# A ring of their own for the raw tiles of the seven-product pairs in the input projection, and an ordinary pair between them

## The chip, the cores and the metric

The kernel runs on one core of one Trainium2 chip. The metric is the device time of one execution in microseconds; three executions of the kernel before gave 2222.35, 2225.07 and 2228.02 us, so the median is 2225.07 us.

## The reference, cut to what matters

The program is a trunk of two layers on 256 tokens of width 2048, all in float32. What the change touches is the first matrix product of each layer, `h @ w_in`: 256 x 2048 by 2048 x 6144. Its columns are the queries, keys and values of two kinds of attention heads.

```python
def hybrid_mixer(h, layer, w_in, w_o, ...):
    proj = h @ w_in                       # (256, 2048) @ (2048, 6144)
    q_sb, k_sb, v_sb, q_d, k_d, v_d = jnp.split(proj, offs, axis=-1)   # 1024 columns each
    o_sb = rms_norm(stick_breaking_attention(q_sb, k_sb, v_sb), sb_out_norm)
    q_d, k_d = partial_rope(q_d), partial_rope(k_d)
    o_d = rms_norm(differential_attention(q1, q2, k1, k2, v_d, lam), diff_subln) * (1 - lam_init)
    return concatenate([o_sb, o_d]) @ w_o

def reference(x, ...):
    for l in range(2):
        x = x + rms_norm(hybrid_mixer(rms_norm(x, pre_mix_norm[l]), ...), post_mix_norm[l])
        x = x + rms_norm(swiglu(rms_norm(x, pre_ffn_norm[l]), ...), post_ffn_norm[l])
    return x
```

## The kernel before, in words

**Split numbers.** Every matrix product is made of three matmuls. A float32 weight tile `raw` is split by ScalarE (ACT) into a rounded part `hi` and by VectorE (DVE) into the rest, `lo = raw - hi`; the activations are split in the same way. `product` (L919 to L924) then issues high by high, high by low and low by high on TensorE (PE), each 128 x 128 stationary against 512 columns.

**Tiles and pairs.** A weight tile holds two blocks of 128 rows, a "K pair" `kp`, and 512 columns: 128 x 1024 numbers, 512 KB. The projection has 12 column chunks of 512, taken two at a time, so it has six column pairs (`PAIRS`, n = 0 to 5), and for each of them it walks through the eight K pairs in the order `IN_ORDER` (n = 0: 0 to 7). An ordinary K pair (`eight_in`) needs two rows x two token tiles x two columns = 8 products, 24 matmuls. A K pair of `IN_SEVEN`, 4 and 5, in the column pairs n = 1 to 4 (`IN_NOW`) is done by a Strassen-like scheme with 7 products, 21 matmuls (`seven_in`, `seven_products`). For this the first and the second column's raw tiles, `g` and `u`, are combined and split on DVE and ACT (`mixed_weights`, L213 on): one addition of 512 columns (L226); the split of `u` into `hi` and `lo` (L222, L223); a difference of 512 columns (L229); an addition of 1024 columns (L230); and the splits of the two results into `Th` and `Tl`. The first tile `g` is also split in the ordinary way (L247, L249). Nearly all of these read or rewrite the raw tiles in place, so both stay in use until the last `Tl`.

**Rings.** All raw tiles of the projection, ordinary or not, come from one ring, `raw`, of 4 buffers. `hi` and `lo` are rings of 6 buffers, three K pairs. `Th` and `Tl` have 2 buffers each in the pool `sums`, which also holds the combined activations (`sh`, `sl`). After the last seven-product pair of a layer `sums` is given up and `late` takes its place. A tile that wants a buffer waits for the last reader of the tile that was in it.

**Queues.** Weight loads go through SyncE's (SP's) DMA queue one after the other (L199 for `raw`), written in the order of `weight_order`, which follows `IN_ORDER`. A load whose buffer isn't free holds up the loads behind it. `weights(i, LOOKAHEAD)` asks for loads and splits four tiles, two K pairs, ahead of the one being multiplied. A scheduler then orders the instructions of each engine; on the chip each engine takes them in that order.

**PSUM banks and attention.** PSUM has eight banks. Four, `acc`, hold the sums of the column pair in work; three, `b`, and one, `o`, serve attention, that runs between the projection's matmuls. A seven-product scheme needs four more sums (`p1`, `p6`, `p7`, `q5`), and takes the three `b` banks and the `o` bank for them. After the last seven-product pair `shared_part` empties these: L959 copies `p1` on ACT, L960 to L963 are additions on DVE that read `p6`, `p7`, `q5` and `q5`.

**The planner.** Attention is written as generators that `tick()` advances; a tick is called once per six matmuls in `eight_in` and four times in seven products, so every K pair has 4 ticks and a column pair 32. `burst` holds the ticks between which the extra sums have the banks; `clear(n)` tells whether n ticks fit before or after it, and after it two more ticks (`SETTLE`) must pass. `banks_for` hands out the `b` banks. The scores of the differential heads (`diff_weights`, L625) take two `b` banks; `flip` transposes a column chunk of queries or keys (L841); `attend` (L546 to L550) multiplies by the values into the bank `o`, from which `norm_pair` makes `on` (L507). The output projection after n = 5 starts a K pair only when the heads that it needs are ready, and lets empty ticks pass until then.

Of the kernel before, what the change touches and what calls it, by code (L numbers as in the profile page):

```python
# [9 lines left out]
F32 = mybir.dt.float32  # L10
F32R = mybir.dt.float32r
# [6 lines left out]
P = 128  # L18
# [7 lines left out]
CW = 512  # L26
# [7 lines left out]
KP_O = (4, 5, 6, 7, 0, 1, 2, 3)  # L34
PAIRS = ((6, 8), (10, 7), (9, 0), (11, 2), (1, 3), (4, 5))
IN_SEVEN = (4, 5)
IN_ORDER = (0, 1, 4, 5, 6, 2, 3, 7)
IN_NOW = ((), IN_SEVEN, IN_SEVEN, IN_SEVEN, IN_SEVEN, ())
SETTLE = 2
SEVEN = (2, 4, 5, 6)  # L40
# [15 lines left out]
def weight_order():  # L56

    order = []

    def queue_pair(name, l, kp, c):  # L60
        order.append((name, l, kp, c))
        return len(order) - 1

    plan = []
    sevens, plain = set(), set()
    for l in range(L):
        lay = {"in": {}, "o": {}, "gate": {}, "up": {}, "down": {}}
        for n, (ca, cb) in enumerate(PAIRS):
            for kp in IN_ORDER if n else range(KT // 2):
                lay["in"][ca, kp] = queue_pair("w_in", l, kp, ca)  # L70
                lay["in"][cb, kp] = queue_pair("w_in", l, kp, cb)
                if kp in IN_NOW[n]:
                    plain.add(lay["in"][cb, kp])
        order_o = [(c, kp) for kp in KP_O for c in (0, 1)]
        order_o += [(c, kp) for c in (2, 3) for kp in range(KT // 2)]
        lay["order_o"] = order_o
        for c, kp in order_o:
            lay["o"][c, kp] = queue_pair("w_o", l, kp, c)
        for c in range(FF // CW):
            for kp in FIRST_ORDER if c == 0 else range(KT // 2):  # L80
                lay["gate"][c, kp] = queue_pair("w_gate", l, kp, c)
                lay["up"][c, kp] = queue_pair("w_up", l, kp, c)
                if kp in (FIRST_SEVEN if c == 0 else SEVEN):
                    sevens.add(lay["up"][c, kp])
        for half in range(2):
            for kp in range(FF // P // 2):
                for c in (2 * half, 2 * half + 1):
                    lay["down"][c, kp] = queue_pair("w_down", l, kp, c)
                if kp in DOWN_SEVEN:
                    sevens.add(lay["down"][2 * half + 1, kp])  # L90
        plan.append(lay)
    return order, plan, sevens, plain
# [14 lines left out]
class Rooms:  # L107


    PASSING = ("a", "ah", "al", "w", "ra", "rb")  # L110
    SUMS = ("Th", "Tl", "sh", "sl")
    LATE = ("mixs", "x", "w_late")

    def __init__(self, tc, name):
# [14 lines left out]
    def tile(self, *args, **kw):  # L129
        for tags, pool in ((self.PASSING, self.passing), (self.SUMS, self.sums), (self.LATE, self.late)):  # L130
            if kw["tag"] in tags:
                return pool.tile(*args, **kw)
        return self.lasting.tile(*args, **kw)
# [7 lines left out]
def kernel(  # L141
# [18 lines left out]
    wpool = ctx.enter_context(tc.tile_pool(name="wpool", bufs=1))  # L160
# [5 lines left out]
    def bank(name):  # L166
        return ps.tile([P, CW], F32, tag="b", bufs=3, name=name)
# [9 lines left out]
    order, plan, sevens, plain = weight_order()  # L177
# [6 lines left out]
    def fetch(upto):  # L184
        while len(raws) < min(upto, len(stream)):
            i = len(raws)
            for j in range(i, min(i + EARLY + 1, mix_raw[3])):
                if j in sevens and j not in sums:
                    summed(j)
            if i in sevens:  # L190
                raws.append(sums[i])
                continue
            if i + 1 in sevens:
                g = mix_raw[0].tile([P, 2, CW], F32, tag="G", bufs=mix_raw[1], name=f"G{i}")
                loads.append(nc.sync.dma_start(g, stream[i]))
                raws.append(g)
                continue
            raw = wpool.tile([P, 2, CW], F32, tag="raw", bufs=4, name=f"raw{i}")
            loads.append(nc.sync.dma_start(raw, stream[i]))  # L199
            raws.append(raw)  # L200

# [2 lines left out]
    def summed(i):  # L204

        sums[i] = mix_raw[0].tile([P, 2, CW], F32, tag="T", bufs=mix_raw[2], name=f"T{i}")
        loads.append(nc.sync.dma_start(sums[i], stream[i]))
        nc.gpsimd.dma_start(sums[i][:, 0, :], stream[i - 1][:, 0, :], accum_op=ALU.add)  # L208

    mix_pool = [None]  # L210
    mix_raw = [None, 0, 0, 0]

    def mixed_weights(i):  # L213

        g, u = raws[i - 1], raws[i]
        hi = wpool.tile([P, 2, CW], F32R, tag="hi", bufs=6, name=f"hi{i}")
        lo = wpool.tile([P, 2, CW], F32R, tag="lo", bufs=6, name=f"lo{i}")
        th = mix_pool[0].tile([P, 3, CW], F32R, tag="Th", bufs=2, name=f"Th{i}")
        tl = mix_pool[0].tile([P, 3, CW], F32R, tag="Tl", bufs=2, name=f"Tl{i}")

        def split(h, l, w):
            nc.scalar.activation(h, w, AF.Copy)  # L222
            nc.vector.tensor_tensor(out=l, in0=w, in1=h.bitcast(F32), op=ALU.subtract)  # L223

        if i in plain:
            nc.vector.tensor_tensor(out=u[:, 0, :], in0=g[:, 0, :], in1=u[:, 0, :], op=ALU.add)  # L226
        split(hi, lo, u)
        t2 = u[:, 1, :]
        nc.vector.tensor_tensor(out=t2, in0=t2, in1=u[:, 0, :], op=ALU.subtract)  # L229
        nc.vector.tensor_tensor(out=g, in0=g, in1=t2.unsqueeze(1).to_broadcast([P, 2, CW]), op=ALU.add)  # L230
        split(th[:, 2, :], tl[:, 2, :], t2)
        split(th[:, 0:2, :], tl[:, 0:2, :], g)
        t1, b22 = ((hi[:, k, :], lo[:, k, :]) for k in range(2))
        t3, t4, t2 = ((th[:, k, :], tl[:, k, :]) for k in range(3))
        return {"b22": b22, "t1": t1, "t2": t2, "t3": t3, "t4": t4}
# [188 lines left out]
    def banks_for(n, ticks, held=False):  # L424

        taken[:] = [until for until in taken if until > clock[0]]
        if len(taken) + n > 3 or not clear(ticks):
            return False
        taken.extend([math.inf if held else clock[0] + 2] * n)
        return True  # L430
# [4 lines left out]
    def start(gen, n=1):  # L435
        running.append([clock[0] + n, gen])
# [355 lines left out]
    def mixer_in(pool, l, rs, xT, mix, mixed):  # L792
# [7 lines left out]
        for n, cc in enumerate(PAIRS):  # L800
            banks = [acc_bank(f"in{l}_{c}_{t}") for t in range(NT) for c in cc]
            mine = IN_NOW[n]
            w, toks = None, {}
# [24 lines left out]
            def flip(c, toks):  # L828
                kind, g = divmod(c, 2)
                st = heads[kind // 3, g]  # L830
                before = {(0, 0): (1, 0), (0, 1): (1, 1)}.get((kind // 3, g))
                while before and heads[before]["scored"] < 2:
                    yield 1
                key = "q" if kind in (0, 3) else "k"
                tT = st[key] = pool.tile([P, 4, S], F32, tag="qk", bufs=4, name=f"{key}T{l}_{c}")
                for t in range(NT):
                    while not banks_for(1, 2):
                        yield 1
                    pb = bank(f"qkT_ps{l}_{c}_{t}")
                    for j in range(4):  # L840
                        nc.tensor.transpose(pb[:, j * P : (j + 1) * P], toks[c, t][:, j * P : (j + 1) * P], ident)  # L841
                    nc.scalar.copy(tT[:, :, t * P : (t + 1) * P], pb.rearrange("p (h q) -> p h q", h=4))
                    yield 2
                st[key + "done"] = True
                if "qdone" in st and "kdone" in st:
                    if kind < 3:
                        start(stick_weights(pool, l, g, st))
                        start(attend(pool, "sb", l, g, st, mix, mixed))
                    else:
                        for j in range(2):  # L850
                            start(diff_weights(pool, l, g, st, j), 1 + 3 * j)
                        start(attend(pool, "df", l, g, st, mix, mixed))
# [3 lines left out]
            else:  # L856
                kps = IN_ORDER if n else tuple(range(KT // 2))
                extra = None
                burst[0] = clock[0] + 4 * kps.index(mine[0]) if mine and n else None
                for j, kp in enumerate(kps):  # L860
# [3 lines left out]
                    if kp in mine:  # L864
# [4 lines left out]
                        if kp == mine[-1]:  # L869
# [4 lines left out]
                            if n + 1 < len(PAIRS) and IN_NOW[n + 1]:  # L874
                                burst[0] = clock[0] + 4 * (len(kps) - 1 - j) + 4 * IN_ORDER.index(IN_NOW[n + 1][0])
                            else:
# [20 lines left out]
            wait = 3  # L897
            for c in cc:
                if c // 2 not in (2, 5):
                    start(flip(c, toks), wait if c // 2 < 3 else wait + 6 + 4 * len(IN_NOW[n + 1]))  # L900
                    wait += 3

    def seven_in(banks, extra, sums, xT, l, cc, kp, first, last):
# [65 lines left out]
    for l in range(L):  # L969
# [130 lines left out]
        for half in range(2):  # L1100
# [69 lines left out]
            for t in range(NT):  # L1170
# [4 lines left out]
                for c in cc:  # L1175
                    for kp in range(nkp - tail, nkp):
# [4 lines left out]
                        for kk in range(2):  # L1181
                            sh, sl = jh[:, kk, t * P : (t + 1) * P], jl[:, kk, t * P : (t + 1) * P]
# [65 lines left out]
```

## Time and profile before

| | before |
|---|---|
| median of three runs | 2225.07 us |
| the profiled execution, its own time | 2224.53 us |
| its span, first to last instruction | 2222.8 us |
| mean granted TensorE clock | 0.996 |
| busy: PE, DVE, ACT, POOL | 2192.6, 1862.7, 1354.5, 135.7 us |
| layer 0, column pairs n = 1 to 5 | about 47.6 to 306.0 us |
| layer 1, column pairs n = 1 to 5 | about 1156.8 to 1410.5 us |

The profile is of one execution. A line of a group gives source line, engine, operation, output <- inputs, count, then busy time and mean duration in ns, then the time that the engine was idle just ahead of these instructions, and what ended it. A line of the waits reads "who <- for whom: us in total, times, longest". A line of the timeline gives the start and the duration in us, and in brackets the idle time before it with its releaser. A line of the windows gives the window, its length, and each engine's busy time and number of instructions, then the granted clock, the share of DMA time and GB/s. Matmuls overlap their neighbours, so the distance of their starts, and not their duration, is what one costs.

### The profile page before, as it was taken

The numbers are of one execution on the slowest core, as the hardware profiler recorded it, in microseconds if no ns is written. First come the engines' busy times: TensorE is split into PE (matmuls) and PEld (weight loads), VectorE is DVE, ScalarE is ACT, GpSimd is POOL, SyncE is SP. The second block draws the span as 40 slices with busy tenths as digits, with TensorE's granted clock in tenths as the row PEclk, the third lists the DMA queues.
The fourth block names the chain that finished last, engine by engine and source line by source line (L and its number), as shares of the span: only waits on it lengthen the run. The fifth ranks groups of instructions, "written<-read, shape, count | busy, mean of one in ns | idle before, by whom it ended". The sixth has DMA issues, their size and how long they took to land. (4 is left out here: it accounts for less than half of the span.)

```text
span 2222.8 us, 28499 instructions
## 1 busy us (share of the span) xinstructions
PE 2192.6 (99%) x10009; PEld 1795.9 (81%) x10009; DVE 1862.7 (84%) x2548; ACT 1354.5 (61%) x2030; POOL 135.7 (6%) x184
## 2 busy tenths in 40 slices
PE   9999999999999999999999999999999999999998
PEld 7778888778888888888888778887778888888886
DVE  7888655899999999989888785559999999989897
ACT  7666664656556656656666556646666556566663
POOL 1100000000000000000020000000000000000000
PEclk9999999999999999999999999999999999999999
DMA  8545555776676675767455455557677667667672
GB/s 298 175 158 184 197 187 182 248 240 220 210 257 214 213 255 188 249 208 241 154 200 171 171 191 178 188 190 256 218 222 234 225 218 239 225 200 241 200 257 96
DMA packets 138079, 466.73 MB, mean 210 GB/s; under 512 B 15824, under 2 KB 16336, under 8 KB 137424
## 3 DMA queue, kind: packets, MB, share of 16 engines
q1 hardware_dynamic: 120512, 430.30, 55.6%
q0 software_dynamic: 15552, 28.32, 7.5%
q10 hardware_dynamic: 1872, 6.31, 0.7%
q8 instruction: 78, 1.28, 0.2%
q14 instruction: 65, 0.53, 0.1%
HBM read 456.47 MB, written 8.39 MB: 209 GB/s over the span
## 5 line engine op out<-in xcount | busy, mean ns | idle before, releaser
L249 DVE TENSOR_TENSOR lo<-raw,hi 128x1024 fp32r<-128x1024 f32 x550 | 662.4, 1224 | 169.6 <-ACT hi L247 168.4
L247 ACT ACTIVATE hi<-raw 128x1024 fp32r<-128x1024 f32 x550 | 569.0, 1054 | 265.5 <-DMA raw<-in_weights_in_turn_dram 96.6
L922 PE MATMUL c<-hi,xF 128*128 128x512 f32 x820 | 321.9, 395 | 5.7 <-DVE w L963 3.6
L923 PE MATMUL c<-lo,xF 128*128 128x512 f32 x820 | 319.8, 390 | 0.0
L924 PE MATMUL c<-hi,xF 128*128 128x512 f32 x820 | 318.2, 390 | 0.0
L208 POOL DMA_DIRECT2D T<-in_weights_in_turn_dram x108 | 94.1, 871 | 1667.3 <-PE c L923 519.0
L922 PEld LDWEIGHTS c<-hi,xF 128*128 128x128 f32 x820 | 153.7, 188 | 40.7 <-DVE w L963 5.7
L1132 PE MATMUL dn<-hi,jh 128*128 128x512 f32 x464 | 180.7, 389 | 0.0
L1133 PE MATMUL dn<-lo,jh 128*128 128x512 f32 x464 | 180.5, 389 | 0.0
L924 PEld LDWEIGHTS c<-hi,xF 128*128 128x128 f32 x820 | 153.9, 188 | 32.2
L923 PEld LDWEIGHTS c<-lo,xF 128*128 128x128 f32 x820 | 154.1, 188 | 31.5 <-DVE lo L249 1.3
L249 DVE TENSOR_TENSOR lo<-G,hi 128x1024 fp32r<-128x1024 f32 x108 | 131.9, 1221 | 26.4 <-ACT hi L247 26.3
L222 ACT ACTIVATE Th<-T 128x512 fp32r<-128x512 f32 x108 | 67.8, 628 | 137.2 <-DVE T L229 126.2
L1135 PE MATMUL dn<-hi,jl 128*128 128x512 f32 x464 | 142.9, 389 | 0.0
L223 DVE TENSOR_TENSOR lo<-T,hi 128x1024 fp32r<-128x1024 f32 x108 | 131.9, 1221 | 10.2 <-ACT hi L222 9.4
L223 DVE TENSOR_TENSOR Tl<-G,Th 128x1024 fp32r<-128x1024 f32 x108 | 132.0, 1222 | 10.0 <-ACT Th L222 10.0
L222 ACT ACTIVATE hi<-T 128x1024 fp32r<-128x1024 f32 x108 | 113.3, 1049 | 39.8 <-PE c L924 21.8
L222 ACT ACTIVATE Th<-G 128x1024 fp32r<-128x1024 f32 x108 | 113.9, 1054 | 36.4 <-DVE G L230 35.1
L230 DVE TENSOR_TENSOR G<-G,T 128x1024 f32<-128x1024 f32 x108 | 132.2, 1224 | 2.1
L922 PE MATMUL in<-hi,xI 128*128 128x512 f32 x328 | 131.7, 403 | 0.2 <-ACT xI L380 0.2
L922 PE MATMUL in<-hi,xT 128*128 128x512 f32 x328 | 131.8, 402 | 0.0
L923 PE MATMUL in<-lo,xI 128*128 128x512 f32 x328 | 128.6, 393 | 0.3 <-DVE lo L249 0.3
(374 smaller groups left out, 4629.8 us busy)
## 6 DMA issues: line engine op xcount, KB each, us to landing
raw<-in_weights_in_turn_dram SPq DMA_DIRECT2D x566, 512.0 KB, 4.5
T<-in_weights_in_turn_dram SPq DMA_DIRECT2D x108, 512.0 KB, 4.8
G<-in_weights_in_turn_dram SPq DMA_DIRECT2D x108, 512.0 KB, 4.6
T<-in_weights_in_turn_dram POOLq DMA_DIRECT2D x108, 256.0 KB, 6.6
away_ffn<-x ACTq DMA_DIRECT2D x8, 512.0 KB, 5.6
xd<-away_ffn SPq DMA_DIRECT2D x8, 512.0 KB, 10.0
xr<-in_x_columns_dram SPq DMA_DIRECT2D x8, 256.0 KB, 6.1
x<-in_x_dram SPq DMA_DIRECT2D x8, 256.0 KB, 6.7
```

The source lines that it names most:

```text
L208: nc.gpsimd.dma_start(sums[i][:, 0, :], stream[i - 1][:, 0, :], accum_op=ALU.add)
L222: nc.scalar.activation(h, w, AF.Copy)
L223: nc.vector.tensor_tensor(out=l, in0=w, in1=h.bitcast(F32), op=ALU.subtract)
L230: nc.vector.tensor_tensor(out=g, in0=g, in1=t2.unsqueeze(1).to_broadcast([P, 2, CW]), op=ALU.add)
L247: nc.scalar.activation(hi, raw, AF.Copy)
L249: rest = nc.vector.tensor_tensor(out=lo, in0=raw, in1=hi.bitcast(F32), op=ALU.subtract)
L922: nc.tensor.matmul(a, sh, hi, start=first, stop=False)
L923: nc.tensor.matmul(a, sh, lo, start=False, stop=False)
L924: nc.tensor.matmul(a, sl, hi, start=False, stop=last)
L1132: nc.tensor.matmul(accs[c, t], sh, hi[:, kk, :], start=first, stop=False)
L1133: nc.tensor.matmul(accs[c, t], sh, lo[:, kk, :], start=False, stop=False)
L1135: nc.tensor.matmul(accs[c, t], sl, hi[:, kk, :], start=False, stop=last)
```

## The change

Four edits go together. First, the raw tiles of a seven-product pair in the input projection come from a ring of their own, `GU`, with 4 buffers in the pool `sums`; the ring `raw` keeps its 4 buffers and serves the ordinary pairs alone. Second, `Th` and `Tl` have one buffer instead of two for the tiles of the input projection. Third, the order of the K pairs becomes 0, 1, 4, 2, 5, 3, 6, 7, so that the ordinary pair 2 stands between the two seven-product pairs and the ordinary pairs 3, 6 and 7 behind them; the order in which the weights lie in memory and are loaded follows. The four extra sums are held from the first product of pair 4 to the last of pair 5, across pair 2. Fourth, the transposes of the differential heads' queries and keys are to start 18 ticks after `wait` instead of 14. The number of products, of loads and of additions stays the same.

```diff
-IN_ORDER = (0, 1, 4, 5, 6, 2, 3, 7)
+IN_ORDER = (0, 1, 4, 2, 5, 3, 6, 7)
...
-    SUMS = ("Th", "Tl", "sh", "sl")
+    SUMS = ("Th", "Tl", "sh", "sl", "GU")
...
-            raw = wpool.tile([P, 2, CW], F32, tag="raw", bufs=4, name=f"raw{i}")
+            if i in plain or i + 1 in plain:
+                raw = mix_pool[0].tile([P, 2, CW], F32, tag="GU", bufs=4, name=f"GU{i}")
+            else:
+                raw = wpool.tile([P, 2, CW], F32, tag="raw", bufs=4, name=f"raw{i}")
             loads.append(nc.sync.dma_start(raw, stream[i]))
...
-        th = mix_pool[0].tile([P, 3, CW], F32R, tag="Th", bufs=2, name=f"Th{i}")
-        tl = mix_pool[0].tile([P, 3, CW], F32R, tag="Tl", bufs=2, name=f"Tl{i}")
+        th = mix_pool[0].tile([P, 3, CW], F32R, tag="Th", bufs=1 if i in plain else 2, name=f"Th{i}")
+        tl = mix_pool[0].tile([P, 3, CW], F32R, tag="Tl", bufs=1 if i in plain else 2, name=f"Tl{i}")
...
-                    start(flip(c, toks), wait if c // 2 < 3 else wait + 6 + 4 * len(IN_NOW[n + 1]))
+                    start(flip(c, toks), wait if c // 2 < 3 else wait + 18)
```

`plain` holds the numbers of the second tiles `u` of the projection's seven-product pairs.

## The prediction

> **What bounds the kernel now.** The page comes first.
>
> ```profile
> span 2222.8 us, 28499 instructions
> PE 2192.6 (99%) x10009; PEld 1795.9 (81%) x10009; DVE 1862.7 (84%) x2548; ACT 1354.5 (61%) x2030; POOL 135.7 (6%) x184
> ```
>
> TensorE is busy for 99% of the span. The change adds and removes no matmul: it can only win back time in which TensorE waits or runs slowly, or add such time. So the next view is the windows over the two stretches that the change touches, the second to sixth column pair of each layer's projection, and two 50 us windows inside them.
>
> ```profile
> 47.60:306.00 258.40, 254.63 (x1227) 207.59 (x1227) 191.28 (x295) 161.84 (x289) 19.43 (x32) 0.99 0.54 183
> 1156.80:1410.50 253.70, 250.83 (x1207) 205.12 (x1206) 187.55 (x291) 156.11 (x282) 17.32 (x25) 0.99 0.52 177
> 100.00:150.00 50.00, 48.20 (x234) 39.37 (x233) 39.50 (x74) 30.56 (x70) 1.95 (x4) 0.97 0.43 148
> 1207.00:1257.00 50.00, 47.68 (x222) 39.37 (x222) 37.83 (x69) 27.56 (x63) 0.00 (x0) 0.93 0.46 153
> ```
>
> Columns are PE, PEld, DVE, ACT, POOL busy, then granted clock, DMA share, GB/s. TensorE idles 258.40 - 254.63 = 3.77 us and 253.70 - 250.83 = 2.87 us, 6.6 us together, and the granted clock dips to 0.97 and 0.93. The waits of PE name all of the idle time:
>
> ```profile
> PE s_df L625 <- DVE w L961: 5.5, 4, 2.3
> PE p_in L922 <- ACT Th L222: 0.8, 1, 0.8
> PE p_in L923 <- DVE Tl L223: 0.4, 1, 0.4
> ```
>
> 5.5 + 0.8 + 0.4 = 6.7 us. The large one is the scores of the differential heads: they take the PSUM banks that the seven-product pairs used, and L961 is the DVE addition that empties the third of these. The timeline shows what such a wait costs:
>
> ```profile
> 55.59 0.39 PE L922 MATMUL in<-hi,xT 128*128 128x512 f32 x1
> 55.82 0.39 PE L923 MATMUL in<-lo,xT 128*128 128x512 f32 x1
> ...
> 125.16 1.00 PE L625 MATMUL s_df<-kT,qT 64*128 64x128 f32 x6 [1.80 <-DVE w L961]
> 126.09 0.79 PE L922 MATMUL in<-hi,xT 128*128 128x512 f32 x1
> 128.39 0.63 PE L548 MATMUL o_df<-v,pT 128*128 128x128 f32 x2
> ...
> 225.55 0.92 PE L625 MATMUL s_df<-kT,qT 64*128 64x128 f32 x6 [0.83 <-DVE w L961]
> ...
> 1228.81 1.65 PE L625 MATMUL s_df<-kT,qT 64*128 64x128 f32 x6 [2.32 <-DVE w L961]
> 1230.38 0.79 PE L922 MATMUL in<-hi,xI 128*128 128x512 f32 x1
> 1232.68 0.63 PE L548 MATMUL o_df<-v,pT 128*128 128x128 f32 x2
> ...
> 1330.35 0.92 PE L625 MATMUL s_df<-kT,qT 64*128 64x128 f32 x6 [0.55 <-DVE w L961]
> ```
>
> Normally a projection matmul starts 0.227 us after the one before (55.59 to 55.82, to three places over a run of them). After the waits of 1.80 and 2.32 us, the five starts from 126.09 to 128.39, and again from 1230.38 to 1232.68, take 2.30 us instead of 5 x 0.227 = 1.14: 1.16 us lost each time, and the scores at 1228.81 take 1.65 instead of 0.92, 0.73 more. So the slow clock costs about 3.1 us, and only after the two long waits. All that can be won back in sight is 6.7 + 3.1 = 9.8 us.
>
> Why is L961 late? DVE and ACT around the first of the waits:
>
> ```profile
> 120.28 1.23 DVE L249 TENSOR_TENSOR lo<-raw,hi 128x1024 fp32r<-128x1024 f32 x1 [0.42 <-ACT hi L247]
> 121.42 0.68 DVE L960 TENSOR_TENSOR w<-p_in,w 128x512 f32<-128x512 f32 x1
> 123.28 1.23 DVE L249 TENSOR_TENSOR lo<-raw,hi 128x1024 fp32r<-128x1024 f32 x1 [1.17 <-ACT hi L247]
> 124.42 0.69 DVE L961 TENSOR_TENSOR w<-p_in,w 128x512 f32<-128x512 f32 x1
> ```
>
> ```profile
> 122.19 1.06 ACT L247 ACTIVATE hi<-raw 128x1024 fp32r<-128x1024 f32 x1 [1.94 <-DMA raw<-in_weights_in_turn_dram]
> ```
>
> L961 stands in DVE's queue behind the `lo` of an ordinary tile, that waits for its `hi` on ACT, and that for its load. The DMA queue's own waits from 100 to 125 us say why the load is late:
>
> ```profile
> SPq L199 <- DVE Tl L223: 12.5, 2, 11.1
> ```
>
> All four `raw` buffers hold the tiles of the two seven-product pairs until their last use, `Tl`; for 11.1 us no load can start.
>
> **The change part by part.** Prices of the splitting work, from the groups by line and form in the first stretch:
>
> ```profile
> L249 DVE TENSOR_TENSOR lo<-raw,hi 128x1024 fp32r<-128x1024 f32 x76 | 91.7, 1232 | 35.7 <-ACT hi L247 35.5
> L223 DVE TENSOR_TENSOR Tl<-raw,Th 128x1024 fp32r<-128x1024 f32 x8 | 9.7, 1217 | 0.2 <-ACT Th L222 0.2
> L230 DVE TENSOR_TENSOR raw<-raw,raw 128x1024 f32<-128x1024 f32 x8 | 9.7, 1217 | 0.1
> L222 ACT ACTIVATE Th<-raw 128x1024 fp32r<-128x1024 f32 x8 | 8.4, 1050 | 0.4 <-DVE raw L230 0.3
> L229 DVE TENSOR_TENSOR raw<-raw 128x512 f32<-128x512 f32 x8 | 5.7, 717 | 0.0
> L226 DVE TENSOR_TENSOR raw<-raw,raw 128x512 f32<-128x512 f32 x8 | 5.6, 696 | 2.5 <-DMA raw<-in_weights_in_turn_dram 2.3
> L223 DVE TENSOR_TENSOR Tl<-raw,Th 128x512 fp32r<-128x512 f32 x8 | 5.5, 682 | 0.2 <-ACT Th L222 0.2
> L222 ACT ACTIVATE Th<-raw 128x512 fp32r<-128x512 f32 x8 | 5.0, 628 | 9.7 <-DVE raw L229 9.7
> ```
>
> *The ring GU.* The four tiles of a column pair's two seven-product pairs no longer sit in `raw`, so the loads of pairs 2, 3 and 6 start when the `lo` of an ordinary pair two pairs earlier is done. The two DVE gaps above, 0.42 + 1.17 = 1.6 us, go. The number of loads, their bytes and the queue (SP's) stay; nothing passes POOL's or ACT's queue. On SP a GU load waits for the previous column pair's `Tl`, long done, so what is queued behind it loses nothing. What is late next is the seven-product work on DVE itself.
>
> *The ordinary pair in between.* A seven-product pair costs DVE 0.70 + 1.23 + 0.72 + 1.22 + 0.68 + 1.22, and 1.23 for its first tile's own `lo`: 7.0 us, while TensorE needs 21 x 0.227 = 4.8. An ordinary pair costs DVE 2 x 1.23 = 2.5 against 24 x 0.227 = 5.4. The scores come two ticks (12 matmuls, 2.7 us) after the last seven-product pair. Before, DVE has 2 x 7.0 + 2 x 0.68 (L960, L961) = 15.4 us to do in 2 x 4.8 + 2.7 = 12.3: 3.1 short. After, 15.4 + 2.5 = 17.9 in 12.3 + 5.4 = 17.7: 0.2 short. That is 2.9 us better, with the 1.6 above 4.5 us, against waits of 0.55 to 2.32. By this the four waits and the slow clock go. Bounds of what stays: 0, or the smallest of them, 0.55, at each of the four places; as 4.5 is twice the longest wait I take the middle, 4 x 0.28 = 1.1 us.
>
> *One buffer for Th and Tl.* New wait: the second seven-product pair's `Th` (ACT), and `Tl` behind it (DVE), cannot be written before TensorE has ended the first one's last product. Behind it on ACT and DVE wait the splits of pairs 3 and 6, and for these TensorE, two pairs later. From that release TensorE has an ordinary pair and then three products, 5.4 + 9 x 0.227 = 7.5 us, before it reads `Th`; the new work takes 0.63 + 1.05 + 1.22 = 2.9 us in a row. The cover is 4.6 us; cost 0. With the cover gone TensorE waits as in the `p_in` rows, 0.8 + 0.4 = 1.2 us a time.
>
> *That first-pair wait of 1.2 us (layer 0).* It is counted in the 9.8; L226 waited for its load (2.3 us over the stretch), which now comes early.
>
> *Attention's window.* By the planner's rules the extra banks are held for 12 ticks of 32 instead of 8, and attention has 18 instead of 22. Counted through, the scores still start 2 ticks after the burst; the output projection still meets no empty tick, and the last stick-breaking head is transposed at tick 216 instead of 214, with 220 the tick that needs it: 4 x 6 x 0.227 = 5.4 us of cover, cost 0. One step comes close: the second attention product of differential group 0 moves to four ticks before a burst, on the bank that q5 takes. q5 follows 36 matmuls, 8.2 us, later. The same step before:
>
> ```profile
> 129.93 0.28 PE L550 MATMUL o_df<-v,pT 128*128 128x128 f32 x1
> 137.74 0.69 DVE L507 TENSOR_TENSOR on_df<-o_df,ors_df 128x512 f32<-128x512 f32 x1
> ...
> 144.16 0.39 PE L550 MATMUL o_df<-v,pT 128*128 128x128 f32 x2
> 148.05 0.69 DVE L507 TENSOR_TENSOR on_df<-o_df,ors_df 128x512 f32<-128x512 f32 x1
> ```
>
> From the last product to the bank's release are 4.2 to 8.2 us, so nothing is lost; one more `lo` in between would cost 1.2 us in each layer. I take 0; bounds 0 to 2.4. `flip` starting 4 ticks later goes with the window. Memory: `sums` grows from 32 to 36 KB a partition, what `late` takes there afterwards; cost 0.
>
> **The sum.** 2224.5 (the profiled execution) - 9.8 + 1.1 = 2215.8 us. The median of the runs, 2225.07, lies 0.55 above that execution, so 2216.4.
>
> **The rivals.**
> *The waits stay.* L961 may now stand behind the `lo` of more pairs, since more of them are ready. For it: `lo` runs between L960 and L961 in the rows above. Against it: 4.5 us of room. It gives 2224.5 less the slow clock at most: 2221 to 2227.
> *The one buffer decides (slower).* For it: DVE is on the edge, 0.2 us short, and ACT and DVE take their work in order, so a `Th` that waits for TensorE holds up the next splits; the eight second pairs could each wait. At 1.2 us each, 9.6 eats the gain: 2225. At 1.80 + 1.16 (the wait at 125.16 with its slow clock) it is 8 x 2.96 = 23.7: 2224.5 - 9.8 + 23.7 = 2238. It decides from (9.8 + 6.7) / 8 = 2.1 us each. Against it: 4.6 us of cover. The Trainium skill (Trainium Kernel Development and Optimization, Best Practices) asks to double-buffer for performance; by it this part loses and GU gains, and the trace of before has no single buffer to weigh it by.
> *The slow clock is not the wait's.* If the clock fell for another reason, the 3.1 us stay: 2219. Against it: it is slow right after 1.80 and 2.32 and normal after 0.83 and 0.55. The Trainium skill (TensorE: Matmul & The Clock Gate, "What's actually happening") puts the fall to half rate after an idle window of about 3.4 us; by that rule waits of 1.8 us would not do it, and the trace disagrees.
>
> **How the numbers follow.** Forecast 0.53, waits stay 0.25, one buffer 0.18, clock 0.04. About 0.3%, 6.7 us, can be told from no change: faster is below 2218.4, slower above 2231.7. Faster 0.53, the same 0.29, slower 0.18. The forecast's own range is 2212 (all 9.8 and some of the short pauses) to 2218.4. The range to hold 8 in 10 takes in the waits that stay and the single buffer's lower prices: 2212 to 2231.
>
> **What would show it.** Right: no PE wait on L961 above 0.55 us, no granted clock under 0.99 in the projection's windows, DMA waits of ACT's `hi` gone there, no SP wait of 11 us on `Tl`. Wrong: new PE waits of `p_in` on `Th` or `Tl` in the second seven-product pairs, or of q5 on L507, above 2 us each; or L961 still behind `lo`.

## The result, and the profile after

The changed kernel takes 2215.14 us (median; 2212.87 to 2216.87) against 2224.6 us for the kernel before (2222.35 to 2228.02). The ratio is 0.9956, with a 95% interval from 0.9942 to 0.9971: 9.5 us less, where 8.7 were forecast.

The page of the profiled execution after:

```profile
span 2213.4 us, 28454 instructions
PE 2185.5 (99%) x10009; PEld 1790.9 (81%) x10009; DVE 1864.0 (84%) x2548; ACT 1354.6 (61%) x2030; POOL 142.2 (6%) x184
```

The work is the same; TensorE's busy time shrank by 7 us, in part because a matmul at half the clock counts as busy for longer. The windows over the second to sixth column pair of both layers (window, length, busy time of the five engines, granted clock, DMA share, GB/s):

```profile
47.60:303.00 255.40, 253.42 (x1235) 206.67 (x1234) 193.47 (x302) 161.79 (x288) 23.50 (x32) 1.00 0.56 191
1153.50:1405.00 251.50, 250.92 (x1228) 205.50 (x1227) 188.59 (x291) 158.52 (x292) 21.39 (x30) 1.00 0.52 175
```

TensorE now idles 1.98 + 0.58 = 2.6 us there instead of 6.6, and the clock no longer dips. The waits of PE in layer 0's window, then in layer 1's:

```profile
PE p_in L925 <- ACT Th L225: 1.3, 1, 1.3
PE o_df L551 <- DVE w L966: 0.4, 1, 0.4
PE pT_df L681 <- DVE w L964: 0.3, 1, 0.3
...
PE o_df L551 <- DVE w L966: 0.4, 1, 0.4
PE pT_df L681 <- DVE w L964: 0.2, 1, 0.2
```

Lines are three higher than before, so L964 is the old L961. The scores `s_df` wait for nothing any more. Where the time went stage by stage, from the first matmul of each stage in the timelines:

| stage | before, us | after, us | ring in the old order (e2), us |
|---|---|---|---|
| layer 0, input projection | 300.7 | 296.6 | 296.3 |
| layer 0, output projection | 95.8 | 97.4 | 95.8 |
| layer 1, input projection | 304.2 | 296.4 | 298.7 |
| layer 1, output projection | 95.8 | 97.4 | 95.8 |

The input projections lost 12.0 us (before rounding), and 3.1 of that came back in the output projections, into which the planner now moves some of attention. The sum, 8.9 us, is nearly the 8.7 forecast. The other stages differ by less than 1.5 us each. The agreement to a few tenths is luck: in a second profiled execution of the same changed kernel (e6, 2210.78 us) the four stages take 783.6 us instead of 787.8, and no wait for a bank is left in them.

And the queues around the first of the old waits. PE, DVE, the DMA queue's waits from 94 to 125 us, and ACT's waits for loads in layer 0's window, after and (last row) before:

```profile
127.56 0.93 PE L628 MATMUL s_df<-kT,qT 64*128 64x128 f32 x8
128.79 0.55 PE L681 MATMUL pT_df<-ident,e_df 128*128 128x128 f32 x3 [0.30 <-DVE w L964]
```

```profile
125.48 0.68 DVE L963 TENSOR_TENSOR w<-p_in,w 128x512 f32<-128x512 f32 x1
127.44 0.69 DVE L229 TENSOR_TENSOR GU<-GU,GU 128x512 f32<-128x512 f32 x1 [1.27 <-DMA GU<-in_weights_in_turn_dram]
128.05 0.68 DVE L964 TENSOR_TENSOR w<-p_in,w 128x512 f32<-128x512 f32 x1
```

```profile
SPq L202 <- DVE s_df L638: 12.7, 2, 11.6
SPq L202 <- DVE Tl L226: 4.2, 3, 2.6
```

```profile
ACT hi L250 <- DMA raw<-in_weights_in_turn_dram: 0.5, 1, 0.5
```

```profile
ACT hi L247 <- DMA raw<-in_weights_in_turn_dram: 15.8, 17, 1.9
```

The ordinary loads come in time: 15.8 us of ACT's waiting shrink to 0.5. But the DMA queue still stands still for 11.6 us, now for a GU buffer (put down to an instruction of DVE that happened to end then), which the scheduler asks for a column pair ahead. And L964 again stands behind an instruction that waits for a load: L229 of the next column pair.

### The profile page after: what moved, and what is told of

It is laid out like the page before. It is cut to its first block, busy times and chain, and to the rows that moved or that the text cites. A ratio compares the mean times of both kernels' runs of the same rounds, so it can differ in the third digit from the quotient of the medians.

```text
span 2213.4 us, 28454 instructions
## 1 busy us (share of the span) xinstructions
PE 2185.5 (99%) x10009; PEld 1790.9 (81%) x10009; DVE 1864.0 (84%) x2548; ACT 1354.6 (61%) x2030; POOL 142.2 (6%) x184
## 4 chain that ended last, share of the span: by engine, by line
PE 78%; DVE 11%; DMA 4%; issue 3%; ACT 3%; SPq 0%; DVEq 0%; ACTq 0%
PE c L925 7%; PE c L926 7%; PE c L927 7%; PE in L925 5%; PE in L927 5%; PE in L926 5%; PE dn L1136 5%; PE dn L1135 5%; PE dn L1138 5%; DVE lo L252 3%; DMA raw<-in_weights_in_turn_dram 3%; PE o L464 3%; PE o L466 3%; PE o L465 3%; DVE Tl L226 2%
## 5 line engine op out<-in xcount | busy, mean ns | idle before, releaser
L252 DVE TENSOR_TENSOR lo<-raw,hi 128x1024 fp32r<-128x1024 f32 x534 | 643.3, 1223 | 161.4 <-ACT hi L250 161.2
L250 ACT ACTIVATE hi<-raw 128x1024 fp32r<-128x1024 f32 x534 | 552.4, 1053 | 235.1 <-DMA raw<-in_weights_in_turn_dram 63.5
L926 PE MATMUL in<-lo,xT 128*128 128x512 f32 x328 | 128.2, 391 | 1.0 <-DVE lo L252 0.8
```

Source lines behind the costliest of these rows:

```text
L250: nc.scalar.activation(hi, raw, AF.Copy)
L252: rest = nc.vector.tensor_tensor(out=lo, in0=raw, in1=hi.bitcast(F32), op=ALU.subtract)
L926: nc.tensor.matmul(a, sh, lo, start=False, stop=False)
```

## The experiments

First theory: the change wins by two parts, the ring (loads) and the pair in between (DVE time), and the single buffer is free because that pair covers it. Rivals: one part does it all; or the waits only show that DVE is behind.

### e1: the new order alone

```diff
-IN_ORDER = (0, 1, 4, 5, 6, 2, 3, 7)
+IN_ORDER = (0, 1, 4, 2, 5, 3, 6, 7)
-... wait + 6 + 4 * len(IN_NOW[n + 1]))
+... wait + 18)
```

> The kernel before with the new order of the K pairs (0, 1, 4, 2, 5, 3, 6, 7) and the later transposes alone; the raw tiles still share one ring of four, Th and Tl keep two buffers. Theory (both parts count, the order by 2.9 us of DVE time per burst, the ring by the 1.6 us of DVE gaps): the order alone brings the waits on L961 from 1.80, 0.83, 2.32, 0.55 us to under 0.8 each, the slow clock goes, the time is 2216 to 2219. Rival 'only the late loads matter, so the ring does it all': the loads still wait for Tl and L961 stays 1 us or more behind, 2221 to 2226.

2220.4 us, ratio 0.9978 (0.9967 to 0.9989): half of the gain, between the theory and its rival. The slow clock is gone from this trace, but bank waits of 3.7 us in all are left in the two projections (on `s_df`, `pT_df` and `o_df`), each 0.8 or less. DVE at the first place:

```profile
126.55 1.23 DVE L249 TENSOR_TENSOR lo<-raw,hi 128x1024 fp32r<-128x1024 f32 x1 [0.95 <-ACT hi L247]
127.69 0.68 DVE L960 TENSOR_TENSOR w<-p_in,w 128x512 f32<-128x512 f32 x1
128.43 1.23 DVE L249 TENSOR_TENSOR lo<-raw,hi 128x1024 fp32r<-128x1024 f32 x1
129.57 0.68 DVE L961 TENSOR_TENSOR w<-p_in,w 128x512 f32<-128x512 f32 x1
```

A `lo` still waits 0.95 us for its `hi` ahead of L960, and another stands between L960 and L961.

### e2 and e5: the ring in the old order

```diff
-    SUMS = ("Th", "Tl", "sh", "sl")
+    SUMS = ("Th", "Tl", "sh", "sl", "GU")
...
+            if i in plain or i + 1 in plain:
+                raw = mix_pool[0].tile([P, 2, CW], F32, tag="GU", bufs=4, name=f"GU{i}")
...
-        th = ... bufs=2
-        tl = ... bufs=2
+        th = ... bufs=1 if i in plain else 2
+        tl = ... bufs=1 if i in plain else 2
```

By the sizes of its tiles `sums` takes 36 KB a partition with a ring of four and single buffers, as much as `late` takes there afterwards; with two buffers for both `Th` and `Tl` it would be 48 KB. So e2 holds two parts of the change, the ring and the single buffers; no run has the ring without them.

> The kernel before with the ring GU and single buffers for Th and Tl, in the old order, so that the two seven-product pairs stand next to each other. Theory: the loads come early, but the cover of the single buffer is gone: TensorE reaches the second pair's Th 2.0 us after the first pair's last product, and the new Th and Tl take 2.9 us in a row at the least, so each of the eight second pairs waits 0.9 to 3 us, 7 to 24 us in all, with slow clock behind the longer ones: 2225 to 2250, slower than before or the same. Rival 'the single buffer costs nothing anywhere and the ring does it all': 2215 to 2219.

2215.31 us, ratio 0.9958 (0.9941 to 0.9974): the whole gain of the change. My theory fell here: with the two seven-product pairs side by side the second pair doesn't wait for its single buffer. PE's waits in layer 0's window are one row, and DVE has no gap ahead of L964:

```profile
PE p_in L925 <- ACT Th L225: 1.1, 1, 1.1
```

```profile
121.00 0.68 DVE L963 TENSOR_TENSOR w<-p_in,w 128x512 f32<-128x512 f32 x1
121.60 1.21 DVE L252 TENSOR_TENSOR lo<-raw,hi 128x1024 fp32r<-128x1024 f32 x1
122.73 0.68 DVE L964 TENSOR_TENSOR w<-p_in,w 128x512 f32<-128x512 f32 x1
```

The `lo` is still in between, but its tile is there. The order of PE's instructions in this trace shows what covers the single buffer. Behind the second pair's first matmuls on `Th` the scheduler put a later product that needs neither `Th` nor `Tl` (`in<-hi,shin`) and two matmuls of the next ordinary pair, all ahead of the first matmul that needs the wide part of `Tl`. That part is done just in time:

```profile
118.70 0.74 PE L925 MATMUL p_in<-Th,shin 128*128 128x512 f32 x2
119.75 0.40 PE L925 MATMUL in<-hi,shin 128*128 128x512 f32 x1
...
120.68 0.39 PE L925 MATMUL in<-hi,xT 128*128 128x512 f32 x1
120.91 0.40 PE L926 MATMUL in<-lo,xT 128*128 128x512 f32 x1
121.14 0.50 PE L926 MATMUL p_in<-Tl,shin 128*128 128x512 f32 x1
```

```profile
119.86 1.22 DVE L226 TENSOR_TENSOR Tl<-GU,Th 128x1024 fp32r<-128x1024 f32 x1
```

New theory: the ring alone wins the waits back, and the order adds nothing to it. So e2's kernel ran again beside the changed one.

> The ring GU and single buffers in the old order once more, beside the changed kernel on the same chip. New theory (the ring alone wins it back, the order is worth nothing once the ring is there): within 2 us of the changed kernel, both about 9 to 10 us below the kernel before. Rival 'the ordinary pair in between adds its own part': 3 us or more above the changed kernel.

> The changed kernel itself, beside the ring in the old order. Both theories: 0.9956 of the kernel before, within 0.001; what differs is the ring's place beside it.

The ring in the old order: 2216.13 us, 0.9959 (0.9945 to 0.9974). The change: 2215.73 us, 0.9952 (0.9938 to 0.9966). Within 0.4 us; once the ring and the single buffers are there, no part of the pair in between can be seen. Which of these two does it in the old order, this comparison doesn't tell; e7 has the single buffers by themselves.

### e3: the change without the ring

```diff
 # e1, and
-        th = ... bufs=2
-        tl = ... bufs=2
+        th = ... bufs=1 if i in plain else 2
+        tl = ... bufs=1 if i in plain else 2
```

> The new order with single buffers for Th and Tl, without the ring: the change less the ring. Theory: the single buffer is covered by the ordinary pair (4.6 us), so it is within 3 us of the order alone, 2216 to 2221, and its p_in waits on Th and Tl are under 2 us in all. Rival 'the single buffer costs': 5 us or more above the order alone.

2221.56 us, 0.998 (0.9971 to 0.999), against 2220.4 for the order alone: within 3 us as the theory said, half a microsecond above the range it named. The p_in wait on `Th` is 1.7 us, one place. The change with its ring is at 0.9952 (0.9938 to 0.9966, e6): in the new order the ring is worth about 6 us, and the two intervals don't touch.

### e4: only the start of attention, two ticks later

```diff
-SETTLE = 2
+SETTLE = 4
```

> The kernel before with attention's window opened 4 instead of 2 ticks after the burst (SETTLE), nothing else: the scores come 2.7 us later, after L961 on all four places, while rings, order and buffers stay. Theory: what is to be won back is these waits and the slow clock behind them, 5.5 + 3.1 us, so 2224.6 - 8.6 = 2216, within 2 us, with DVE and the loads as late as before. Rival 'the waits only show that DVE is behind, TensorE waits for it elsewhere': 2222 to 2226.

2217.54 us, 0.9968 (0.9959 to 0.9978): 7 to 8 us won with rings, order and buffers as they were. It holds the theory's main claim: what the projection had to give back is mostly the collision of attention's scores with L961. The first place:

```profile
126.58 0.93 PE L625 MATMUL s_df<-kT,qT 64*128 64x128 f32 x8
128.51 0.49 PE L548 MATMUL o_df<-v,pT 128*128 128x128 f32 x2 [1.00 <-DVE w L963]
```

The scores run without a wait, and the next product to need a bank waits 1.00 us for L963 instead: it is less than the 1.80 before, and no slow clock follows. Over both layers 2.4 us of such waits stay, of 5.5.

### e7: the single buffer alone

```diff
-        th = ... bufs=2
-        tl = ... bufs=2
+        th = ... bufs=1 if i in plain else 2
+        tl = ... bufs=1 if i in plain else 2
```

> The kernel before with single buffers for Th and Tl and nothing else: old order, raw tiles in one ring of four. It prices the single buffer where no ordinary pair covers it. New theory (the scheduler puts other matmuls of TensorE ahead of those that need the second Th and Tl, so nothing waits on the chip): 2222 to 2228, the same as before. Rival, the step of the prediction by which the cover is the ordinary pair: the second pairs wait 0.9 us or more each, 8 x 0.9 = 7 us or more slower, 2232 and up.

2218.29 us, 0.9968 (0.9957 to 0.9979): faster than before, which neither expectation had. The DMA queue's waits from 100 to 125 us are those of the kernel before, and yet PE waits on no L961. DVE shows why: after the row of the queue, its rows in the kernel before and then in e7.

```profile
SPq L199 <- DVE Tl L223: 12.1, 3, 11.1
```

```profile
116.37 1.22 DVE L223 TENSOR_TENSOR Tl<-raw,Th 128x1024 fp32r<-128x1024 f32 x1
117.50 2.35 DVE L249 TENSOR_TENSOR lo<-raw,hi 128x1024 fp32r<-128x1024 f32 x2
```

```profile
116.40 2.35 DVE L249 TENSOR_TENSOR lo<-raw,hi 128x1024 fp32r<-128x1024 f32 x2
118.67 1.82 DVE L223 TENSOR_TENSOR Tl<-raw,Th 128x512 fp32r<-128x512 f32 x2
120.53 0.69 DVE L960 TENSOR_TENSOR w<-p_in,w 128x512 f32<-128x512 f32 x1
121.32 0.69 DVE L961 TENSOR_TENSOR w<-p_in,w 128x512 f32<-128x512 f32 x1
122.11 1.23 DVE L249 TENSOR_TENSOR lo<-raw,hi 128x1024 fp32r<-128x1024 f32 x1
```

The second pair's `Tl` comes later, behind two `lo` and just ahead of L960, and the `lo` of the late tiles comes behind L961 instead of ahead of it (before, L961 ran at 124.42). So the late load by itself costs nothing that this run shows; it costs when the work that waits for it stands ahead of L961 in DVE's queue. The time from the start of the last seven-product matmul to the end of this addition, in the order n = 1 to 4 of layer 0, then of layer 1, worked out from the timelines of each kernel:

| kernel | us | mean |
|---|---|---|
| before | 0.92 4.24 3.45 3.27, 4.19 4.76 3.07 3.00 | 3.4 |
| e1, order alone | 1.25 3.34 2.70 2.82, 4.13 3.28 2.40 3.67 | 2.9 |
| the change | 0.99 2.85 1.49 1.01, 1.49 2.74 1.49 1.01 | 1.6 |
| e2, ring in the old order | 1.34 1.47 1.16 1.16, 1.23 1.49 1.14 1.19 | 1.3 |
| e7, single buffer alone | 1.12 -0.24 0.78 0.78, 0.79 -0.27 0.79 0.79 | 0.6 |

The old waits are the second and the fourth of each layer. e7 beats e2 in this column, and it too has no bank wait left; its time can't be told from e2's (0.9957 to 0.9979 against 0.9941 to 0.9974). So in the old order the single buffers by themselves take L961 out of the way, and what the ring adds to them there isn't shown.

### e8 and e11: two and three buffers in the ring

```diff
 # e2, and
-                raw = mix_pool[0].tile(... tag="GU", bufs=4 ...)
+                raw = mix_pool[0].tile(... tag="GU", bufs=2 ...)     # e11: 3
```

> The ring in the old order with two buffers instead of four: one seven-product pair at a time. New theory (what counts is that the ordinary loads don't wait for Tl): the second pair's tiles load only after the first pair's Tl, 4.5 us of loading and then the whole of the mixing on DVE, while TensorE has 4.8 us in the first pair; the second pair is late by 3 us or more in each of the eight places, 2230 or more. Rival 'separation alone is enough, two buffers do': 2215 to 2219.

> The ring in the old order with three buffers, the base of the run with a third seven-product pair, and the point between two buffers (2225) and four (2216). Theory: the second pair's second tile loads when the first pair's first tile is free, after Tl, so it is late by about as much as with two buffers: 2221 to 2226. Rival 'three do': 2215 to 2218.

Two buffers: 2225.07 us, 0.9999 (0.9989 to 1.0008). Three: 2218.16 us, 0.9974 (0.9964 to 0.9984). Four: 0.9959. The kernel to set beside these is e7, the same single buffers without a ring, at 0.9968: a ring of two is slower than none, and rings of three and four can't be told from none in the old order. With two, L964 is as early as in e2 (mean 1.4 us), but the second pair's tiles come late. Of PE's waits over the whole run:

```profile
PE p_in L925 <- ACT Th L225: 4.8, 5, 1.5
```

I had the cause right and the price too high: 1.5 us at the most instead of 3 or more each, and five waits in all. Three buffers are in the rival's range but for 0.2 us, against my expectation.

### e9: attention one tick earlier

```diff
-SETTLE = 2
+SETTLE = 1
```

> The kernel before with attention's window opened one tick after the burst instead of two: the scores come 1.36 us earlier, so each of the four waits on L961 should grow by as much, to about 3.2, 2.2, 3.7 and 1.9 us. It prices a wait and asks when the clock falls. If the clock falls after a wait of 1.8 us or more inside a stretch of 3.4 us or more without a 512-column matmul, all four places run slow behind the wait: 4 x 1.36 + 2 x 1.2 to 2 = 8 to 9 us above the kernel before, 2232 to 2234. If only an unbroken wait of 3.4 us does it, one place at most is slow and the time is 2228 or less.

2230.45 us, 1.0026 (1.0015 to 1.0038): slower, by less than expected. The planner laid attention out anew and the waits did not simply grow: in the trace two of them are on L961 (1.22 and 1.36 us) and others on L960 and L507. The trace is of the slowest of the seven executions (2237.31 us). Where the clock falls, it answers otherwise than both rules; see below.

### e10: a third seven-product pair

```diff
 # e11, and
-IN_SEVEN = (4, 5)
+IN_SEVEN = (4, 5, 6)
```

> The ring in the old order with three buffers, and a third seven-product pair (K pair 6) in the column pairs n = 1 to 4: 8 x 3 matmuls less, 8 x 0.68 = 5.4 us less on TensorE, against 8 x 4.6 us more on DVE, which is busy for 81% of the projection. Theory (DVE sets the end of a burst): three adjacent pairs ask 21 us of DVE in 14.3 us of TensorE, the third pair waits for Th and Tl or L961 is late again, the gain is eaten: 2214 to 2226. Rival 'DVE has room over a whole column pair': 2209 to 2213, faster than the changed kernel.

2238.7 us, 1.0068 (1.0053 to 1.0083): worse than the theory's range. The window of layer 0's column pairs:

```profile
47.60:317.40 269.80, 261.54 (x1220) 204.64 (x1219) 206.78 (x319) 168.19 (x295) 20.58 (x32) 1.00 0.54 180
```

TensorE idles 8.3 us in it, and the stage is 14 us longer than in the change although 12 matmuls fewer run there. How much of that is DVE's load and how much attention being moved, this run doesn't separate.

No kernel tried beats the change; the ring in the old order equals it.

## Why the prediction was right or wrong

**What bounds the kernel: right, with one term too small.** All that the stretches lost was put at 9.8 us, 6.7 of waits and 3.1 of slow clock. e4 wins 7 to 8 of it by moving the scores alone, and the change 8.9 over both projections. But the slow clock was counted only as far as the five matmuls of 512 columns. The windows of the kernel before show a granted clock of 0.50 for 3.41 us and for 6.83 us, and the attention products behind those five start 0.42 us apart in them (128.39 to 128.81) instead of 0.22:

```profile
125.87:129.28 3.41, 3.41 (x11) 2.71 (x11) 3.39 (x8) 0.47 (x1) 0.00 (x0) 0.50 0.81 273
1228.38:1235.21 6.83, 6.41 (x24) 5.27 (x24) 5.19 (x11) 1.23 (x2) 0.00 (x0) 0.50 0.71 245
```

```profile
128.81 0.62 PE L549 MATMUL o_df<-v,pT 128*128 128x128 f32 x2
...
129.49 0.39 PE L548 MATMUL o_df<-v,pT 128*128 128x128 f32 x2
129.71 0.39 PE L549 MATMUL o_df<-v,pT 128*128 128x128 f32 x2
...
1235.09 0.53 PE L924 MATMUL in<-hi,xI 128*128 128x512 f32 x1
```

Two such steps behind the first place and six behind the second (1232.68 to 1235.09) add about 1.4 us: the slow clock costs about 4.5 us, not 3.1. With it the two results come out: in e4 5.5 - 2.4 + 4.5 = 7.6 us, in the change 6.6 - 2.6 + 4.5 = 8.5 against the 8.9 measured.

**The ring: the right mechanism, sized too small, and never run by itself.** I gave it the two DVE gaps, 1.6 us, and thought that this was not enough for the longest wait, 2.32. In the changed kernel's order it is worth about 6 us (e3 against e6). Not only the gaps go; ACT no longer waits for loads (15.8 to 0.5 us in the change), so the work ahead of L961 is done earlier. In the old order the four waits go with the ring and the single buffers together (e2: L964 ends 4.24 - 1.47 = 2.8 us earlier at the first place), but also with the single buffers alone (e7). There ACT still waits 20.1 us for loads in layer 0, against 4.1 in e2: late loads cost TensorE nothing that can be seen as long as L961 doesn't stand behind them.

**The pair in between: wrong.** The step that set 15.4 us of DVE work against 12.3 of TensorE's, and 17.9 against 17.7 after, counted the `lo` of one ordinary pair and none of the others. Given more time, DVE takes more in ahead of L961: three `lo` in a row and L229 of the next column pair. The room was not 4.5 us: by the table L964 is 3.4 - 1.6 = 1.8 us earlier on average than L961 was, and it ends later than in e2; in the profiled execution `pT_df` still waits 0.30 us for it. e1, which has this step alone, wins half; beside the ring and the single buffers it adds nothing (e5 and e6).

**The single buffer: cost 0, right; the reason, not the one that counts.** I had PE in the written order and let the ordinary pair cover the chain of 2.9 us. e2 has no such pair and no such wait: the scheduler fills the place. In the old order the single buffer even gains 6 to 7 us (e7), because the second `Tl` moves back and takes L961 out from behind the late `lo`. In the new order it gains nothing (e3 against e1). So the slower rival, that this buffer decides, falls.

**The first wait in layer 0, 1.2 us: wrong.** It is 1.3 us after (0.9 in e6). The GU tiles land in time and L229 no longer waits; ACT waits for L232 on DVE, which comes behind the `lo` of ordinary pairs. What I had taken for the load was DVE's order.

**Attention's window: mostly right.** TensorE idles no more than 0.1 us in either output projection, and q5 does not wait on L507 (L510 now). That 1.5 us of attention in each layer move into the output projection I did not price; it only moves work, as TensorE's busy time shows, 95.7 us before and 97.2 after in each output projection.

**GU on the DMA queue: wrong in the detail.** "Loses nothing" held for the time, but a GU buffer a column pair ahead stops the queue for 11.6 us, where I expected that such a wait would go.

**The remaining 1.1 us: near, by luck.** What is left of the bank waits is 0.3 + 0.4 + 0.2 + 0.4 = 1.3 us, on `pT_df` and `o_df` instead of `s_df`; in e6 nothing is left of them.

The close agreement of 2216.4 with 2215.1 therefore rests on the list of what could be won back, not on the split between its causes, and on two errors that cancel: the slow clock was put 1.4 us too low, and 2.6 us of waits stayed instead of 1.1. The path, attention's scores behind L961 and that behind work that waits for loads, is what the runs bear out.

## What to carry to other kernels

Read a wait of the bounding engine to the end of its chain: here TensorE waited for a bank, the bank for an addition, the addition for its place in DVE's queue behind a subtraction, and that for a load whose buffer a slow consumer held. A ring of its own for tiles that are held long frees the ones that pass through quickly; but each link can be cut, and moving the addition ahead (e7) or the taker of the bank back (e4) won two thirds of the gain or more without any new buffer. Before a buffer or an order is credited, run it alone; here the ring was only run together with the single buffers, and in the old order those by themselves won about three quarters of what the two won together.

## What the runs showed of the hardware

The clock. The prediction held that it falls after a wait of 1.8 us, and that the Trainium skill's rule (TensorE: Matmul & The Clock Gate, "What's actually happening": an idle window of about 3.4 us, running freely) disagrees. The runs don't bear out a threshold on the single wait. In the changed kernel's feed-forward part a longer wait, between wide matmuls, leaves the clock as it was:

```profile
496.35 0.50 PE L925 MATMUL c<-hi,xF 128*128 128x512 f32 x1 [2.11 <-DVE w L966]
496.92 0.39 PE L927 MATMUL c<-hi,xF 128*128 128x512 f32 x1
```

In e9 a wait of 1.22 us is followed by slow work, four scores in 1.65 us and a matmul of 0.79:

```profile
126.87 1.65 PE L625 MATMUL s_df<-kT,qT 64*128 64x128 f32 x4 [1.22 <-DVE w L961]
128.45 0.79 PE L922 MATMUL in<-hi,xT 128*128 128x512 f32 x1
```

What the two slow places of the kernel before have in common with this one is a long stretch without any 512-column matmul: 3.87 and 5.03 us there, 3.19 here and 2.50 around the wait of 2.11. But in e4 stretches of 3.94 and 4.38 us, with waits of 1.00 and 1.44, run at full clock. Idle time and small matmuls within a window of some three microseconds, placed by chance, would fit all of these, and the Trainium skill's free-running window would too.

The granted clock in the traces shows such windows. It is 0.50 for 3.41 or for twice 3.41 us, and the falls lie whole multiples of that apart: in the kernel before 1228.38 - 125.87 = 1102.51 us, 323 times 3.4133; in e9, with falls at 126.49, 1239.24 and 1290.44, 326 and 15 times. A fall does not wait for the end of a wait either: in e9 the scores behind a wait of 1.36 us still take 0.92, and the matmuls are slow only from 1239.24 on.

```profile
1237.70 0.92 PE L625 MATMUL s_df<-kT,qT 64*128 64x128 f32 x4 [1.36 <-DVE w L961]
...
1239.43 0.63 PE L922 MATMUL in<-hi,xI 128*128 128x512 f32 x1
```

In the 3.41 us ahead of the two falls of the kernel before TensorE is busy for 1.61 and 1.52 us, so the window need not be empty:

```profile
122.46:125.87 3.41, 1.61 (x12) 1.05 (x10) 2.59 (x3) 2.79 (x4) 0.00 (x0) 1.00 0.87 324
1224.97:1228.38 3.41, 1.52 (x9) 0.99 (x7) 1.88 (x3) 2.31 (x3) 0.00 (x0) 1.00 1.00 372
```

In the change the 3.41 us from 492.70, with most of the wait of 2.11, hold 1.54 us of wide matmuls, and no fall follows. So the busy share alone doesn't decide; what counts as idle stays open.

That the bank waits brought the slow clock is shown: where they go or shrink (the change, e2, e4, e7), no stretch of slow matmuls is left in the projections. The other executions point the same way: the mean granted clock is 0.997 or less in 44 of the 61 of the kernel before that ran beside the experiments, and in 3 of the 38 of these kernels (e5 and e6 counted in).
